# The front of a hybrid conv/DeltaNet layer: adaLN vectors in three column parts, the first scale summed by TensorE, the rows of x scaled ahead, four strips opened on the first part

## The chip, the cores and the metric

One core of one Trainium2 chip runs one program. The engines are TensorE (PE, with its weight loads PEld), VectorE (DVE), ScalarE (ACT), GpSimd (POOL) and SyncE (SP), which issues most transfers. The metric is the device time of one execution in microseconds. All inputs and the output are float32 in HBM.

## The reference

The layer takes x (2048 rows of 1024) and a vector c. Six vectors of 1024 come from `silu(c) @ w_ada + b_ada`; the first two of them, with a gain, shift and scale the normalized rows of x ahead of the large product with `w_in`:

```python
c_act = jax.nn.silu(c)
mod = c_act @ w_ada[layer] + b_ada[layer]
shift_m, scale_m, gate_m, shift_f, scale_f, gate_f = jnp.split(mod, N_MOD, axis=-1)
h = adaln(x, g_norm_mix[layer], shift_m, scale_m)     # rms_norm(x, gain) * (1 + scale) + shift
p = h @ w_in[layer]
gate_b, gate_c, h_conv, q, k, v, z, a, bt = jnp.split(p, split_at, axis=-1)
...
ya = gate_b * causal_depthwise_conv(gate_c * h_conv, conv_w_mix[layer])     # then a group norm
qkv = jax.nn.silu(causal_depthwise_conv(jnp.concatenate([q, k, v], axis=-1), conv_w_qkv[layer]))
...
o = chunked_gated_delta_rule(q, k, v, g_dec, beta)    # g_dec and beta from a and bt, per row and head
y = jnp.concatenate([ya, yb], axis=-1) @ w_out[layer]  # yb: o, normalized, times silu(z)
x = x + gate_m[:, None, :] * y
h = adaln(x, g_norm_ffn[layer], shift_f, scale_f)
x = x + gate_f[:, None, :] * ((jax.nn.silu(gt) * up) @ w_down[layer])
return adaln(x, g_norm_final, shift_o, scale_o)
```

## The kernel before

The sequence is cut into four blocks of 512 rows. In each block the mixing stage computes, for every strip of 128 columns of `w_in`, a product over eight k rows of 128 (`proj`, line 321 through `dmm`): the transposed, normalized h is held as two float32r tiles, `hTh` and `hTl` (a rounded part and the rest), the weight strip as `whi` and `wlo` (`split_w`, lines 388 and 390), and each k takes three matmuls of 128x512, so a strip takes 24. I call these the dense matmuls. The strips come in the order k, q, v, z (four heads each), then twelve for the convolution branch, then the product with `w_out`. Behind the mixing stage stand the feed-forward products.

Beside the dense matmuls run side chains, written as generators and resumed from `tick`: `head_chain` (the decay values `g` from a small product with the columns `wab`, then per head a masked k k^T), `q_chain`, `v_chain`, `diagonal_chain`, a triangular solve on VectorE that goes through DRAM twice, `level_chain`, `chunk_chain` (the recurrence over four chunks of a block) and `out_chain`, whose results (`ybs`) the third of the four steps of the product with `w_out` waits for.

A planner, `Clock`, sets the order. It keeps an estimated time for every instruction as it is recorded (`note`), decides from it when a side chain is resumed, and from the point at which `pinned` is set, each engine's instructions are put in order of these estimated times (`pin`). For a transfer it reckons 1.2 us, then bytes over a rate, then 0.8 us; the rate is line 140's. Before `pinned` is set the program's order counts, as the tile framework schedules it. `pinned` is set in block 0 when the q strips begin.

Banks of PSUM come from two pools of four, `dense_ps` (`pd`) and `misc_ps` (`pm`). The dense strips use the first; side chains, transposes and small sums use the second.

The front is everything ahead of block 0's loop. `Gm` (1 + scale, times gain) and `Sm` (shift) are needed as columns of 128 values, one per k. `part_norm` (line 726) does this in two column parts, k 0 to 4 and k 5 to 7. For each part `part_mod` (line 705) loads eight row pieces of `w_ada` (128 x 640, then 128 x 384), and VectorE multiplies each by one value of `cs` = silu(c) per partition and adds it to `acc` (lines 711, 713); `col_sums` (line 465) sums over partitions with a TensorE product with ones (line 468, two passes a call). This is done first for scale, then for shift. Every second piece also takes one step of `load_norm_steps` (line 530): load 128 rows of x, sum their squares (line 521), two small POOL steps (lines 515, 516) and scale them (line 537). Then `transpose_k` (line 544) turns x for one k through TensorE, and `scale_split` (lines 548 to 550) applies `Gm` and `Sm` and splits the result into `hTh` and `hTl`.

After the first part the small product with `wab` (`proj_ab`, lines 751 and 752) runs over k 0 to 4, and strips 0 and 1 of head group k do so too (`part_proj`, line 743); strips 2 and 3 follow behind the second part's preparation. `pre` holds the opened strips; block 0's loop finishes them over k 5 to 7. The first four `wlo` are made by VectorE once and by POOL three times (`lo_engines`).

Of the kernel before, what the change touches and what calls it, by code (L numbers as in the profile page):

```python
# [53 lines left out]
class Clock:  # L54
# [74 lines left out]
    def note(self, i):  # L129
# [9 lines left out]
        if op == "DMACopy":  # L139
            cost = min(a.free_size() * a.partition_size() for a in outs + ins) * 4 / 240e3  # L140
            begin = self.fit([eng], start, 0.45) - 0.45
# [68 lines left out]
def layer_kernel(ctx, tc, x, c, w_ada, b_ada, w_ada_final, b_ada_final, g_norm_mix, g_norm_ffn, g_norm_final,  # L210
# [19 lines left out]
    def dense_ps():  # L230
        return pd.tile([P, 512], F32, name="pd")
# [233 lines left out]
    def col_sums(acc, n):  # L465
        ps = dense_ps()
        for j in range(n):
            mm(ps[:, j * 16:(j + 1) * 16], acc[:, j * P:(j + 1) * P], ones[:, :16], start=True, stop=True)
        return ps[:, :n * 16].rearrange("p (j n) -> p j n", n=16)[:, :, 0]
# [71 lines left out]
    def transpose_k(tiles, k):  # L541
        ps = misc_ps()
        for i in range(CH):
            nc.tensor.transpose(ps[:, i * P:(i + 1) * P], tiles[i][:, k * P:(k + 1) * P], ident)
        return ps
# [126 lines left out]
    with ExitStack() as actx:  # L672
# [27 lines left out]

        xt0, pre = [], []
        xsteps = load_norm_steps([x[i * P:(i + 1) * P, :] for i in range(CH)], ap_, "kq", xt0)

        def part_mod(c0, js, slots):
            n = len(js) * P
            acc = ap_.tile([P, D], F32, name="zs" if c0 else "gate_m")[:, :n]
            for k in range(KD):
                raw = next(slots)[:, :n]
                nc.sync.dma_start(raw, w_ada[k * P:(k + 1) * P, c0 + js[0] * P:c0 + js[0] * P + n])
                if k == 0:  # L710
                    nc.vector.tensor_scalar_mul(acc, raw, cs[:, 0:1])
                else:
                    nc.vector.scalar_tensor_tensor(acc, raw, cs[:, k:k + 1], acc, op0=ALU.mult, op1=ALU.add)
                if k % 2:
                    next(xsteps, None)
            return acc

        def part_slots(names):
            while True:
                for n in names:  # L720
                    if n == "wraw":
                        yield wr.tile([P, D], F32, name=n)
                    elif n == "ym":
                        yield ap_.tile([P, BLK], F32, name=n, bufs=8)
                    else:
                        yield ap_.tile([P, D], F32, name=n)

        def part_norm(js, names):
            g, sh = Gm[:, js[0]:js[-1] + 1], Sm[:, js[0]:js[-1] + 1]
            b_g, gain, b_s = (col[n][:, js[0]:js[-1] + 1] for n in ("b_cm", "g_mix", "b_sm"))  # L730
            slots = part_slots(names)
            nc.scalar.copy(g, col_sums(part_mod(D, js, slots), len(js)))
            nc.gpsimd.tensor_add(g, g, b_g)
            nc.gpsimd.tensor_scalar_add(g, g, 1.0)
            nc.gpsimd.tensor_mul(g, g, gain)
            acc = part_mod(0, js, slots)
            if not pre:
                fill(4)
            early = [transpose_k(xt0, k) for k in js[:3]]
            nc.vector.tensor_add(sh, col_sums(acc, len(js)), b_s)  # L740
            for i, k in enumerate(js):
                scale_split(early[i] if i < len(early) else transpose_k(xt0, k), k, Gm, Sm, *hT)

        def part_proj(h):
            pre.append((ready.popleft(), dense_ps()))
            clock.kept.add(pre[-1][1].name)
            proj(pre[h][1], pre[h][0], *hT, ks=range(5))

# [4 lines left out]

        lo_engines.extend([nc.vector] + [nc.gpsimd] * 3)
        big = ["kd", "vt", "yah", "yal"]
        part_norm(range(5), ["wraw"] * 4 + big)

# [4 lines left out]
        nc.gpsimd.tensor_sub(wabs[:, :, 8:16], wab, wabs[:, :, 0:8].bitcast(F32))  # L762

        ps_ab = misc_ps()
        clock.kept.add(ps_ab.name)
        proj_ab(ps_ab, range(5))
        for h in range(2):
            part_proj(h)
        part_norm(range(5, KD), ["ym"] * 8 + big)
        for h in range(2, NH):  # L770
            part_proj(h)
        nc.sync.dma_start(ck[:, P:], cst[:, P:])
# [19 lines left out]
        for b in range(NB):  # L792
# [382 lines left out]
            if b:  # L1175
                ps_ab = misc_ps()
            proj_ab(ps_ab, range(0 if b else 5, KD))
            clock.kept.discard(ps_ab.name)
# [3 lines left out]
            for key, c0, dstT in (("k", 2048, kT), ("q", 1536, qT), ("v", 2560, None)):  # L1182
                clock.pinned = clock.pinned or key == "q"
                for h in range(NH):
                    m = (c0 - 1536) // P + h
                    if pre:
                        w, ps = pre.pop(0)
                        proj(ps, w, hh, hl, range(5, KD))
                        clock.kept.discard(ps.name)
                        fill(h + 1)  # L1190
                    else:
                        w, ps = next_w(), dense_ps()
                        proj(ps, w, hh, hl)
# [637 lines left out]
```

## Time and profile before

| | |
|---|---|
| three timed runs | 2441.77, 2443.42, 2444.44 us (median 2443.42) |
| profiled execution | 2441.17 us, of which the span from the first to the last instruction is 2439.4 |
| mean granted TensorE clock | 0.985 |
| moved | 336.98 MB, mean 138 GB/s |

A row of the page's first part is an engine's busy time, its share of the span and its instructions. In a table by stage a row gives the stretch, its length, busy time and instructions of each engine named, the granted clock, the share of the DMA engines and GB/s. In the timeline a row is the start, the time it took, engine, line, operation, output and inputs with their shapes, the count of merged instructions, and in brackets the idle time before it and what ended it. A wait is given as who waited for whom, the total, the number of times and the longest. Matmul times overlap, so the pace of a stream is read from start to start.

### The profile page before, as it was taken

Reading aid. Unit: us, or ns where it says so; the run is one execution under the profiler, and the core shown is the slowest. Engines: PE = TensorE matmul, PEld = TensorE weight load, DVE = VectorE, ACT = ScalarE, POOL = GpSimd, SP = SyncE. Lnnn points to the kernel's source line nnn. Section 1 sums busy time; section 2 is a strip of 40 time slices with the busy share of each in tenths; the row PEclk is TensorE's granted clock in tenths of the full one; section 3 lists DMA queues with packets and bytes.
Section 4 is the critical chain, followed back from the end, with each engine's and each line's share of the span. In section 5 each row is a group of like instructions: output and inputs, shape, how many; then the busy total and the mean of one; then the engine's idle time right before and its main releaser. Section 6 shows DMA issues by size and latency. Waiting matters only on the chain. (4 is left out here: it accounts for less than half of the span.)

```text
span 2439.4 us, 30808 instructions
## 1 busy us (share of the span) xinstructions
PE 2344.2 (96%) x11243; PEld 1935.6 (79%) x11243; DVE 1769.4 (73%) x2577; ACT 1044.8 (43%) x1841; POOL 592.6 (24%) x655
## 2 busy tenths in 40 slices
PE   5899899999999999988999999999999999999997
PEld 4688788887888788876878888878888877888786
DVE  5788669886887687777565565876656558878887
ACT  4543554344644474346543333533333323323345
POOL 2340344033602261221000000000000035434448
PEclk9899999999999999998999999999999999999999
DMA  7443355625562346136673243753333364333433
GB/s 249 112 117 87 95 173 158 183 95 151 152 160 87 113 121 161 51 123 196 193 226 117 87 120 99 246 168 106 108 92 116 100 240 156 117 115 126 134 132 144
DMA packets 397535, 336.98 MB, mean 138 GB/s; under 512 B 39476, under 2 KB 338749, under 8 KB 397383
## 3 DMA queue, kind: packets, MB, share of 16 engines
q1 hardware_dynamic: 397126, 334.91, 45.1%
q8 instruction: 88, 1.44, 0.2%
q14 instruction: 65, 0.52, 0.1%
q10 hardware_dynamic: 256, 0.10, 0.0%
HBM read 261.55 MB, written 73.41 MB: 137 GB/s over the span
## 5 line engine op out<-in xcount | busy, mean ns | idle before, releaser
L388 ACT CAST whi<-wraw 128x1024 fp32r<-128x1024 f32 x278 | 291.5, 1049 | 379.9 <-PE pd L321 180.7
L390 DVE TENSOR_TENSOR wlo<-wraw,whi 128x1024 fp32r<-128x1024 f32 x275 | 339.6, 1236 | 109.3 <-ACT whi L388 101.7
L321 PE MATMUL pd<-hTh,whi 128*128 128x512 f32 x896 | 365.2, 408 | 3.5 <-ACT hTh L549 2.6
L321 PE MATMUL pd<-hTl,whi 128*128 128x512 f32 x896 | 351.6, 392 | 2.7 <-DVE hTl L550 2.7
L321 PE MATMUL pd<-hTh,wlo 128*128 128x512 f32 x896 | 351.7, 392 | 0.0
L321 PEld LDWEIGHTS pd<-hTh,whi 128*128 128x128 f32 x896 | 169.7, 190 | 36.4 <-ACT hTh L549 2.7
L321 PEld LDWEIGHTS pd<-hTh,wlo 128*128 128x128 f32 x896 | 169.2, 189 | 36.5
L321 PEld LDWEIGHTS pd<-hTl,whi 128*128 128x128 f32 x896 | 170.0, 190 | 34.2 <-DVE hTl L550 3.1
L1505 POOL TENSOR_TENSOR wraw<-wraw 128x1024 f32<-128x1024 f32 x2 | 4.9, 2468 | 780.3 <-DMA wraw<-in_w_down_dram 780.3
L1459 DVE TENSOR_TENSOR sg<-sg,pd 128x512 f32<-128x512 f32 x44 | 30.2, 687 | 171.4 <-PE pd L321 165.0
L1699 DVE TENSOR_TENSOR acc<-acc,pd 128x512 f32<-128x512 f32 x192 | 127.5, 679 | 30.8 <-PE pd L321 30.8
L1582 ACT CAST xh<-ra 128x640 fp32r<-128x640 f32 (+1 forms) x88 | 62.5, 719 | 185.7 <-PE pm L321 142.8
L1160 DVE SCALAR_TENSOR_TENSOR cv<-pd,pcb,cv 128x511 f32<-128x511 f32 (+2 forms) x176 | 131.5, 747 | 4.9
L1591 POOL TENSOR_TENSOR xl<-ra,xh 128x640 fp32r<-128x640 f32 (+1 forms) x40 | 66.1, 1654 | 160.8 <-ACT xh L1582 160.8
L1699 DVE TENSOR_TENSOR acc<-acc,pm 128x512 f32<-128x512 f32 x120 | 81.6, 681 | 18.4 <-PE pm L321 17.8
L1299 POOL TENSOR_TENSOR cv<-cv,cb 128x512 f32<-128x512 f32 x32 | 52.2, 1644 | 164.7 <-DVE cv L1298 140.3
L321 PE MATMUL pd<-whi,ym 128*128 128x512 f32 x256 | 87.9, 404 | 1.5 <-ACT ym L1149 1.5
L1628 POOL TENSOR_TENSOR wraw<-wraw 128x512 f32<-128x512 f32 x40 | 69.6, 1761 | 43.3 <-DMA wraw<-in_w_down_dram 32.6
L321 PE MATMUL pd<-S2h,whi 128*128 128x512 f32 x176 | 69.5, 395 | 3.1 <-ACT whi L388 3.1
L321 PE MATMUL pd<-S3h,t3h 128*128 128x512 f32 x176 | 69.0, 392 | 2.9 <-ACT sg L1445 2.9
L321 PE MATMUL pd<-S2h,wlo 128*128 128x512 f32 x176 | 69.6, 396 | 2.2 <-DVE wlo L390 2.2
L321 PE MATMUL pd<-A22h,whi 128*128 128x512 f32 x176 | 69.6, 395 | 2.3 <-DVE sg L1459 2.2
(457 smaller groups left out, 6228.0 us busy)
## 6 DMA issues: line engine op xcount, KB each, us to landing
wraw<-in_w_in_dram SPq DMA_DIRECT2D x112, 512.0 KB, 4.0
wraw<-in_w_gate_up_dram SPq DMA_DIRECT2D x88, 512.0 KB, 3.7
ra<-act SPq DMA_DIRECT2D x80, 448.0 KB, 3.8
act<-S SPq DMA_DIRECT2D x80, 256.0 KB, 2.2
act<-act SPq DMA_DIRECT2D x68, 256.0 KB, 2.2
wraw<-in_w_ada_dram SPq DMA_DIRECT2D x32, 512.0 KB, 3.7
wraw<-in_w_out_dram SPq DMA_DIRECT2D x32, 512.0 KB, 3.8
wraw<-in_w_down_dram SPq DMA_DIRECT2D x22, 512.0 KB, 3.8
```

What stands on the lines that cost most here:

```text
L321: mm(*args, **kw)
L388: nc.scalar.copy(hi, raw)
L390: (lo_engines.popleft() if lo_engines else nc.vector).tensor_sub(lo, raw, hi.bitcast(F32))
L1160: nc.vector.scalar_tensor_tensor(cv[:, n - t:], u[:, :BLK - n + t], taps[t], cv[:, n - t:], op0=ALU.mult, op1=ALU.add)
L1299: nc.gpsimd.tensor_add(yo, yo, xr)
L1459: nc.vector.tensor_add(s5[i], s5[i], a[i])
L1505: nc.gpsimd.tensor_mul(r, r, first_w["gate"])
L1582: nc.scalar.copy(hi, raw[:, c0:c1, :])
L1591: eng.tensor_sub(lo, raw, hi.bitcast(F32))
L1628: nc.gpsimd.tensor_mul(r[:, hs], r[:, hs], gate_f[:, hs])
L1699: nc.vector.tensor_add(accs[s, u][:, ns], accs[s, u][:, ns], ps)
```

## The change

The front is written anew. There are three column parts: k 0 to 2, 3 to 5, 6 and 7. In the first part the scale is not summed by VectorE: for each piece of `w_ada` TensorE multiplies three 128x128 blocks with one column of `cs` and adds up over the eight pieces in PSUM. The other sums are made as before. `Gm` is finished by two VectorE operations instead of a copy on ScalarE and three steps on POOL. The rows of x are loaded ahead of and behind the first eight pieces, and their squares are summed and scaled in one go (`x_norm`). All transposes of a part stand ahead of its `Sm`. The four strips of head group k are all opened on the first part and continued on the second, and `proj_ab` runs over k 0 to 5 behind the second part. All four first `wlo` are VectorE's. `col_sums` takes its bank from `misc_ps`. The planner's rate for transfers goes from 240 to 380, `pinned` is set at the k strips instead of the q strips, and block 0's first q strip takes a bank of `misc_ps`.

```diff
-            cost = min(a.free_size() * a.partition_size() for a in outs + ins) * 4 / 240e3
+            cost = min(a.free_size() * a.partition_size() for a in outs + ins) * 4 / 380e3
...
     def col_sums(acc, n):
-        ps = dense_ps()
+        ps = misc_ps()
...
+        PARTS = range(3), range(3, 6), range(6, KD)
+        pre = []
+        pairs = [ap_.tile([P, 2, D], F32, name="kq", bufs=2) for _ in range(2)]
+        xt0 = [pairs[i // 2][:, i % 2, :] for i in range(CH)]
+
+        def x_load(i):
+            nc.sync.dma_start(xt0[i], x[i * P:(i + 1) * P, :])
+
+        def x_norm():
+            ss = []
+            for i in range(CH + 1):
+                if i < CH:
+                    ss.append(sum_squares(xt0[i]))
+                if i:
+                    nc.scalar.activation(xt0[i - 1], xt0[i - 1], AF.Identity, scale=ss[i - 1])
+
+        def part_slots():
+            while True:
+                for _ in range(8):
+                    yield ap_.tile([P, BLK], F32, name="ym", bufs=8)
+                for n in ("kd", "vt", "yah", "yal"):
+                    t = ap_.tile([P, 4, BLK], F32, name=n)
+                    for i in range(4):
+                        yield t[:, i]
+
+        def part_raw(c0, js):
+            for k in range(KD):
+                raw = next(slots)[:, :len(js) * P]
+                nc.sync.dma_start(raw, w_ada[k * P:(k + 1) * P, c0 + js[0] * P:c0 + (js[-1] + 1) * P])
+                yield k, raw
+
+        def part_sums(c0, js):
+            n = len(js)
+            if c0 and js[0] == 0:
+                ps = misc_ps()
+                for k, raw in part_raw(c0, js):
+                    for j in range(n):
+                        mm(ps[:, j:j + 1], raw[:, j * P:(j + 1) * P], cs[:, k:k + 1], start=k + j == 0,
+                           stop=k == KD - 1, skip_group_check=True)
+                return ps[:, :n]
+            acc = ap_.tile([P, D], F32, name="zs" if c0 else "gate_m")[:, :n * P]
+            for k, raw in part_raw(c0, js):
                 if k == 0:
                     nc.vector.tensor_scalar_mul(acc, raw, cs[:, 0:1])
                 else:
                     nc.vector.scalar_tensor_tensor(acc, raw, cs[:, k:k + 1], acc, op0=ALU.mult, op1=ALU.add)
+            return col_sums(acc, n)
+
+        def part_norm(js):
             g, sh = Gm[:, js[0]:js[-1] + 1], Sm[:, js[0]:js[-1] + 1]
             b_g, gain, b_s = (col[n][:, js[0]:js[-1] + 1] for n in ("b_cm", "g_mix", "b_sm"))
-            nc.scalar.copy(g, col_sums(part_mod(D, js, slots), len(js)))
-            nc.gpsimd.tensor_add(g, g, b_g)
-            nc.gpsimd.tensor_scalar_add(g, g, 1.0)
-            nc.gpsimd.tensor_mul(g, g, gain)
-            acc = part_mod(0, js, slots)
+            if js[0] == 0:
+                x_load(0)
+                x_load(1)
+            nc.vector.tensor_add(g, part_sums(D, js), b_g)
+            nc.vector.scalar_tensor_tensor(g, g, 1.0, gain, op0=ALU.add, op1=ALU.mult)
+            if js[0] == 0:
+                x_load(2)
+                x_load(3)
+                x_norm()
+            sums = part_sums(0, js)
             if not pre:
-                fill(4)
-            early = [transpose_k(xt0, k) for k in js[:3]]
-            nc.vector.tensor_add(sh, col_sums(acc, len(js)), b_s)
-            for i, k in enumerate(js):
-                scale_split(early[i] if i < len(early) else transpose_k(xt0, k), k, Gm, Sm, *hT)
+                fill(NH)
+            early = [transpose_k(xt0, k) for k in js]
+            nc.vector.tensor_add(sh, sums, b_s)
+            for ps, k in zip(early, js):
+                scale_split(ps, k, Gm, Sm, *hT)
...
-        lo_engines.extend([nc.vector] + [nc.gpsimd] * 3)
-        big = ["kd", "vt", "yah", "yal"]
-        part_norm(range(5), ["wraw"] * 4 + big)
+        slots = part_slots()
+        lo_engines.extend([nc.vector] * 4)
+        part_norm(PARTS[0])
+        for h in range(NH):
+            part_start()
+            proj(pre[h][1], pre[h][0], *hT, ks=PARTS[0])
+        part_norm(PARTS[1])
...
+        for h in range(NH):
+            proj(pre[h][1], pre[h][0], *hT, ks=PARTS[1])
         ps_ab = misc_ps()
         clock.kept.add(ps_ab.name)
-        proj_ab(ps_ab, range(5))
-        for h in range(2):
-            part_proj(h)
-        part_norm(range(5, KD), ["ym"] * 8 + big)
-        for h in range(2, NH):
-            part_proj(h)
+        proj_ab(ps_ab, range(6))
+        part_norm(PARTS[2])
...
-            proj_ab(ps_ab, range(0 if b else 5, KD))
+            proj_ab(ps_ab, range(0 if b else 6, KD))
...
-                clock.pinned = clock.pinned or key == "q"
+                clock.pinned = clock.pinned or key == "k"
...
-                        proj(ps, w, hh, hl, range(5, KD))
+                        proj(ps, w, hh, hl, PARTS[2])
...
-                        w, ps = next_w(), dense_ps()
+                        w, ps = next_w(), misc_ps() if b == 0 and key == "q" and h < 1 else dense_ps()
```

The change moves instructions at three places that matter below. In these rows a name like `L544` is the line, then come operation, output and inputs, shape of the output and count.

TensorE at the opening, before (`kq` holds the rows of x, `zs` and `gate_m` the sums for scale and shift, `pd` and `pm` are PSUM banks):

```order
L362 MATMUL pm<-ck,ht 128x64
L544 MATMUL pm<-ck,kq 128x128 x12
L468 MATMUL pd<-ones_r,zs 128x16 x5
L544 MATMUL pm<-ck,kq 128x128 x4
L468 MATMUL pd<-ones_r,gate_m 128x16 x5
L321 MATMUL pd<-hTh,whi 128x512 x2
```

and with the change, the same stretch (line 738 is the product in `part_sums`, `ym` a piece of `w_ada`):

```order
L362 MATMUL pm<-ck,ht 128x64
L738 MATMUL pm<-cs,ym 128x1 x24
L468 MATMUL pm<-ones_r,gate_m 128x16 x3
L544 MATMUL pm<-ck,kq 128x128 x12
L321 MATMUL pd<-hTh,whi 128x512 x2
```

The transposes have moved behind the column sums of shift, and the 24 narrow products stand in place of the scale's column sums.

VectorE at the decay chain of block 0, before (`cv` is a strip's convolution, `sp_*` and `g` the decay values, `wlo` a weight strip's lower part):

```order
L845 COPY cv<-pm 16x512
L454 SCALAR_TENSOR_TENSOR wraw<-wraw,cs 128x1024
L885 RECIPROCAL beta<-beta 128x16
L1158 TENSOR_SCALAR cv<-pd,pcb 128x512
L866 TENSOR_SCALAR sp_s<-sp_e 128x16
L390 TENSOR_TENSOR wlo<-wraw,whi 128x1024
L867 RECIPROCAL sp_s<-sp_s 128x16
L1160 SCALAR_TENSOR_TENSOR cv<-pd,pcb,cv 128x511
L868 TENSOR_TENSOR sp_s<-sp_s,sp_e 128x16
L390 TENSOR_TENSOR wlo<-wraw,whi 128x1024
L870 TENSOR_TENSOR sp_z<-sp_s 128x16
```

and with the change (25 more lines stand ahead of the loop, so line 866 is 891 now):

```order
L870 COPY cv<-pm 16x512
L1183 TENSOR_SCALAR cv<-pd,pcb 128x512
L1185 SCALAR_TENSOR_TENSOR cv<-pd,pcb,cv 128x511
L891 TENSOR_SCALAR sp_s<-sp_e 128x16
L892 RECIPROCAL sp_s<-sp_s 128x16
L893 TENSOR_TENSOR sp_s<-sp_s,sp_e 128x16
L895 TENSOR_TENSOR sp_z<-sp_s 128x16
L897 TENSOR_SCALAR sp_p<-sp_z 128x16
L899 SCALAR_TENSOR_TENSOR sp_p<-sp_p,sp_z 128x16 x7
L900 SCALAR_TENSOR_TENSOR sp_p<-sp_p,sp_s 128x16
```

The small operations stand together; the convolutions and the `wlo` that were between them come behind.

TensorE at the end of block 0, before (`ch` is a chunk's intermediate, `ym` an output of `out_chain`; the last row is the transpose in the last chunk's `out_chain`, line 1143):

```order
L1116 MATMUL pm<-ch,kd 128x128 x4
L1118 MATMUL pm<-ch,E 128x128 x4
L321 MATMUL pd<-whi,ym 128x512
L321 MATMUL pd<-wlo,ym 128x512
L321 MATMUL pd<-whi,ym 128x512 x2
L321 MATMUL pd<-wlo,ym 128x512
L321 MATMUL pd<-whi,ym 128x512 x2
L321 MATMUL pd<-wlo,ym 128x512
L321 MATMUL pd<-whi,ym 128x512
L1143 MATMUL pm<-ck,ch 128x128 x4
```

and with the change (that transpose is line 1168 now):

```order
L1168 MATMUL pm<-ck,ch 128x128 x4
L321 MATMUL pd<-whi,ym 128x512
L321 MATMUL pd<-wlo,ym 128x512
L321 MATMUL pd<-whi,ym 128x512
L1141 MATMUL pm<-ch,kd 128x128 x4
L1143 MATMUL pm<-ch,E 128x128 x4
L321 MATMUL pd<-whi,ym 128x512
L321 MATMUL pd<-wlo,ym 128x512
L321 MATMUL pd<-whi,ym 128x512
L1168 MATMUL pm<-ck,ch 128x128 x4
```

Three dense matmuls instead of nine stand between the last chunk's products and its transpose.

More of the change, by code (lines that the diff above doesn't have):

```diff
@@ L696, in layer_kernel @@
         state = ap_.tile([P, NH * P], F32, name="state")
[L701 to L706, printed above, removed]
-            for k in range(KD):
-                raw = next(slots)[:, :n]
-                nc.sync.dma_start(raw, w_ada[k * P:(k + 1) * P, c0 + js[0] * P:c0 + js[0] * P + n])
+        PARTS = range(3), range(3, 6), range(6, KD)
[20 more added lines that the diff above has]
+        def part_raw(c0, js):
+            for k in range(KD):
+                raw = next(slots)[:, :len(js) * P]
[12 more added lines that the diff above has]
+            for k, raw in part_raw(c0, js):
                 if k == 0:
@@ L713, in part_mod, with part_start @@
                     nc.vector.scalar_tensor_tensor(acc, raw, cs[:, k:k + 1], acc, op0=ALU.mult, op1=ALU.add)
[L714 to L728, printed above, removed]
+            return col_sums(acc, n)
+        def part_norm(js):
             g, sh = Gm[:, js[0]:js[-1] + 1], Sm[:, js[0]:js[-1] + 1]
             b_g, gain, b_s = (col[n][:, js[0]:js[-1] + 1] for n in ("b_cm", "g_mix", "b_sm"))
-            slots = part_slots(names)
-            nc.scalar.copy(g, col_sums(part_mod(D, js, slots), len(js)))
-            nc.gpsimd.tensor_add(g, g, b_g)
-            nc.gpsimd.tensor_scalar_add(g, g, 1.0)
-            nc.gpsimd.tensor_mul(g, g, gain)
-            acc = part_mod(0, js, slots)
-            if not pre:
-                fill(4)
-            early = [transpose_k(xt0, k) for k in js[:3]]
-            nc.vector.tensor_add(sh, col_sums(acc, len(js)), b_s)
-            for i, k in enumerate(js):
-                scale_split(early[i] if i < len(early) else transpose_k(xt0, k), k, Gm, Sm, *hT)
-        def part_proj(h):
+            if js[0] == 0:
[8 more added lines that the diff above has]
+            sums = part_sums(0, js)
+            if not pre:
+                fill(NH)
[3 more added lines that the diff above has]
+                scale_split(ps, k, Gm, Sm, *hT)
+        def part_start():
             pre.append((ready.popleft(), dense_ps()))
             clock.kept.add(pre[-1][1].name)
-            proj(pre[h][1], pre[h][0], *hT, ks=range(5))
         def proj_ab(ps, ks):
```

## The prediction

> **What bounds the kernel now.** I read the page's busy shares first, then a table by stage of the first 102 us, then TensorE's waits there, then the timeline.
>
> ```profile
> PE 2344.2 (96%) x11243; PEld 1935.6 (79%) x11243; DVE 1769.4 (73%) x2577; ACT 1044.8 (43%) x1841; POOL 592.6 (24%) x655
> ```
> ```profile
> 0.00:32.00 32.00, 8.95 (x39) 1.00 0.97 338
> ...
> 70.30:85.00 14.70, 6.94 (x18) 0.54 0.54 150
> 85.00:101.95 16.95, 16.95 (x75) 1.00 0.11 31
> ```
> ```profile
> PE pm L544 <- ACT kq L537: 13.1, 4, 5.1
> PE pm L889 <- DVE g L878: 6.5, 1, 6.5
> ```
>
> TensorE is busy 96% of the span, so time is won only where it stands idle or slow. The stage table (columns: length, TensorE busy, granted clock, DMA share, GB/s) shows two such places: up to 32 us, where it has almost no work, and 70.3 to 85, busy 6.94 of 14.70 us at clock 0.54. The second has a cause of its own: the decay chain (`head_chain`) needs `g` from VectorE, and TensorE waits 6.5 us for it. The change touches both. I follow the kernel to one mark, the first transpose of a k strip in `head_chain` (101.95), which stands behind 177 dense matmuls, and compare the work left.
>
> ```profile
> 7.59 0.34 PE L362 MATMUL pm<-ck,ht 64*128 64x64 f32 x1 [2.29 <-DMA ht<-in_g_norm_ffn_dram]
> ...
> 18.89 2.26 PEld L468 LDWEIGHTS pd<-ones_r,zs 128*128 128x128 f32 x10
> ...
> 30.41 1.03 ACT L388 CAST whi<-wraw 128x1024 fp32r<-128x1024 f32 x1
> ...
> 31.35 0.59 ACT L549 CAST hTh<-pm 128x512 fp32r<-128x512 f32 x1
> ...
> 31.82 0.76 ACT L548 ACTIVATE pm<-pm,Sm,Gm 128x512 f32<-128x512 f32 x1
> 31.97 0.69 DVE L550 TENSOR_TENSOR hTl<-pm,hTh 128x512 fp32r<-128x512 f32 x1 [1.10 <-ACT hTh L549]
> ...
> 31.99 1.22 PE L321 MATMUL pd<-hTh,whi 128*128 128x512 f32 x2 [2.56 <-ACT hTh L549]
> 32.50 1.05 ACT L388 CAST whi<-wraw 128x1024 fp32r<-128x1024 f32 x1
> ...
> 43.17 0.42 DVE L711 TENSOR_SCALAR gate_m<-kd,cs 128x384 f32<-128x384 f32 x1
> 43.50 0.61 DVE L713 SCALAR_TENSOR_TENSOR zs<-ym,cs,zs 128x384 f32<-128x384 f32 x1
> 44.03 0.61 DVE L713 SCALAR_TENSOR_TENSOR gate_m<-vt,cs,gate_m 128x384 f32<-128x384 f32 x1
> ```
> ```profile
> 48.58 0.73 PE L468 MATMUL pd<-ones_r,zs 128*128 128x16 f32 x6
> ...
> 81.33 0.63 PE L321 MATMUL pd<-hTl,whi 128*128 128x512 f32 x1
> 81.76 0.63 PE L321 MATMUL pd<-hTh,wlo 128*128 128x512 f32 x1
> ...
> 99.45 0.39 PE L321 MATMUL pd<-hTh,whi 128*128 128x512 f32 x1
> 99.68 0.39 PE L321 MATMUL pd<-hTl,whi 128*128 128x512 f32 x1
> ...
> 101.95 0.60 PE L829 MATMUL pm<-ck,kq 128*128 128x128 f32 x4
> ```
>
> From these rows come start-to-start prices. A dense matmul: 0.43 us slow (81.33 to 81.76), 0.23 fast. A short pass with a 128x128 weight load: 2.26/10, some 0.22 slow, 0.73/6 = 0.12 fast; a call of L468 is two passes. VectorE on a 128x384 piece: 0.33 for the first, 0.53 for the others. ScalarE: cast of a strip 0.94, split cast 0.47, scale 0.68.
>
> **The change, part by part.**
>
> *First scale.* Its eight DVE steps become 24 TensorE calls with one column: 48 passes. One column is not in the trace; bounds are half of a slow pass (fast, 0.11) and a slow one, and I take slow, 0.213, since TensorE is otherwise idle there. They stand behind L362, which ends at 7.9, so 7.9 + 48 x 0.213 = 18.1. Before, its column sums ended at 18.89 + 2.26 = 21.2, and a copy and three POOL steps followed. Now two small VectorE operations make `Gm` by 18.6.
>
> *First shift.* VectorE can start at 18.6; 0.33 + 7 x 0.53 = 4.0 gives 22.7. Its data stand behind x (2.1 MB) and the scale's pieces (1.57 MB), 5.2 MB with its own:
>
> ```profile
> 2.00:10.00 8.00, 0.58 (x2) 0.36 (x2) 3.21 (x4) 2.93 (x6) 0.68 (x1) 1.00 0.96 343
> 10.00:22.00 12.00, 5.29 (x22) 4.39 (x22) 8.21 (x10) 6.24 (x9) 2.55 (x7) 1.00 1.04 404
> ```
>
> At 343 GB/s to 10 us and 404 after (last column), they land at about 16.3, so transfers are hidden; at 300 GB/s for the narrower rows they would land at 19.5, still ahead of the last step. Then six passes (24.1) and twelve transposes on TensorE, the first four ending near 25.0; ScalarE's norms of x are over by 19 and no longer on the path. Scale 0.68, a strip's cast 0.94 that ScalarE's order puts between, split 0.59: **first dense matmul at 27.5, before 31.99**.
>
> *First part on four strips.* ScalarE gives a row k every 0.68 + 0.94 + 0.47 = 2.1 us, so the last `hTh` of three is there at 31.6, `hTl` at 32.6. All four `wlo` are VectorE's now instead of one; they fall into its waits. 36 dense matmuls, slow till about 32.5, end near 38.
>
> *Second part.* VectorE begins its sums only behind that last `hTl`, at 32.6: 16 pieces of 384, four of 256 from the third part that its order mixes in, 2 x 4.0 + 1.3 = 9.4 with the ends, so 42.0. TensorE has nothing dense from 38 to there. Column sums, `Sm`: 42.9. Then 12 transposes, 12 calls of `proj_ab`, 36 dense: 1.4 + 48 x 0.227 = 12.3; I add 1.7, one slow stretch of 3.4 us, because TensorE has stood nearly idle for 3 us. The second part ends at 56.8.
>
> *Third part.* Eight passes 0.9, `Sm` and `Gm` 0.5, scale and split 1.3, the last row's split, `hTl` and calls 1.9: nothing covers this on TensorE but two calls (before, 30 dense matmuls of strips 2 and 3 did). `proj_ab` ends at 61.4, before at 59.6 (next fence: VectorE's copy at 59.65 waits for it). So the earlier start is spent again by here; but at this point 22 dense matmuls of the k strips are left, before 36.
>
> *The decay chain.*
>
> ```profile
> 59.65 0.68 DVE L845 COPY cv<-pm 16x512 f32<-16x512 f32 x1 [2.33 <-PE pm L752]
> ...
> 63.55 0.17 DVE L866 TENSOR_SCALAR sp_s<-sp_e 128x16 f32<-128x16 f32 x1 [0.15 <-ACT sp_e L862]
> ...
> 76.53 0.16 DVE L878 TENSOR_TENSOR g<-sp_p,nexpa 128x16 f32<-128x16 f32 x1
> ```
> ```profile
> 329.75 0.11 DVE L866 TENSOR_SCALAR sp_s<-sp_e 128x16 f32<-128x16 f32 x1
> ...
> 332.77 0.18 DVE L878 TENSOR_TENSOR g<-sp_p,nexpa 128x16 f32<-128x16 f32 x1
> ```
>
> ```profile
> 116.61 1.28 DVE L454 SCALAR_TENSOR_TENSOR wraw<-wraw,cs 128x1024 f32<-128x1024 f32 x1
> ...
> 132.26 0.75 DVE L1158 TENSOR_SCALAR cv<-pd,pcb 128x512 f32<-128x512 f32 x1
> ...
> 136.49 0.69 DVE L918 TENSOR_TENSOR kd<-pm,eg 128x512 f32<-128x512 f32 x1
> ```
>
> The chain's small operations alternate with convolutions here (first fence): 13.0 us from 63.55 to 76.53. The change pins the order one strip group earlier, and VectorE now has them in one piece, as in block 1 (second fence), where this takes 3.0. So `g` is there 6.5 us behind `proj_ab`; but TensorE's order has the fifth strip's `wlo` ahead of the chain's matmuls, and VectorE makes it behind the chain: 8.4. TensorE waits 2 us for that. Before, `g` was there 76.7 - 59.6 = 17.1 behind. From there to the mark remain 78 dense, eight decay matmuls and six small ones, 86 x 0.227 + 0.5 = 20.0; before 25.2, because of the slow clock. VectorE needs 4.2 us for a strip's convolution and `wlo` (132.26 to 136.49) and at most 1.2 for a gate step, TensorE 24 x 0.227 = 5.4, and the first q strip takes a bank of the other pool, so the late convolutions hold up nothing. Mark: 61.4 + 8.4 + 20.0 = 89.8; with 0.7 for the chance of a slow stretch, 90.5, **11.5 earlier**.
>
> *The planner's transfer price* (240 to 380) reorders blocks 0 to 2; block 3's TensorE order around its chains is as before. I price blocks 1 and 2 at nothing, between -3 and +5: by the waits over the whole span TensorE's frequent wait there, for `kT`, was 0.6 us at most.
>
> ```profile
> PE pm L829 <- ACT kq L1198: 2.0, 4, 0.6
> ```
>
> Block 0's end I price:
>
>
> ```profile
> 264.30 3.35 DVE L1232 RECIPROCAL cv<-cv 128x512 f32<-128x512 f32 x1
> ```
> ```profile
> 275.82 2.17 ACT L537 ACTIVATE kq<-kq,ss 128x1024 f32<-128x1024 f32 x2
> ```
> ```profile
> 279.31 1.11 PE L1143 MATMUL pm<-ck,ch 128*128 128x128 f32 x4 [5.72 <-POOL ch L1138]
> ```
>
> The last chunk's output ends on a chain of VectorE, ScalarE and POOL that TensorE awaits. Now the reciprocal comes ahead of that chunk's first step (some 1.3 us shown to TensorE), three norm steps of x precede its squares instead of following (near 1), and 3 instead of 9 dense matmuls cover it (1.4): 3 us, bounds 0 and 6. Sum: -11.5 + 3.0 = **-8.5**.
>
> **The clock.**
>
> ```profile
> 40.00:44.00 4.00, 2.94 (x7) 1.55 (x8) 4.00 (x8) 0.00 (x0) 0.00 (x0) 0.59 0.71 222
> 44.00:48.00 4.00, 4.00 (x18) 2.64 (x17) 3.86 (x8) 0.00 (x0) 0.00 (x0) 0.98 0.53 122
> ```
>
> TensorE came out of a wait here (busy 2.94 of the first 4 us, so at work from about 41.1), and its granted clock was 0.59 in the first stretch and 0.98 in the second: some 3.3 us of work to the full clock. The short passes at 18.9 to 21.2 us were slow, but ran for 2.3 us only. The Trainium skill, "TensorE: Matmul & The Clock Gate", Part 1, says that the clock is halved by default, that about 3.4 us of sustained matmul activity release it, and that an idle window of that length halves it again. The rows agree with that for dense matmuls; whether passes that load 128x128 weights for one column count as such activity, no row shows. If they do, the first scale ends as the first rival has it, if not, as in the sum.
>
> **The rivals.**
> - *The short passes speed up.* Slow for 3.3 us (15 passes), then fast: 7.9 + 3.3 + 33 x 0.12 = 15.2, and all behind comes 2.9 earlier, since the pieces of the shift are there by 16.3: 2432.0. For it: TensorE has work without a break there. Against it: a single column. Chance 0.2.
> - *VectorE bounds block 0* (slower). It is busy 75.06 of the 92.90 us from 59.6 to the solve's first transfer at 152.5 (row below). With the 17.84 us of idle time that it had, starting 1.8 later, the chain is 1.8 later; TensorE then gives its lead back at the block's end and waits 3 longer: +4.8, 2448.2. It decides if VectorE idles over 16 us there; I count 3. Chance 0.09.
> - *The lead is lost in part*, at block ends or to waits of a too hopeful transfer price: -4 to +3, near 2443. Chance 0.16.
> - *Block 0's end gains instead*, with its 5.7 us wait gone: -16, near 2427. Chance 0.1.
>
> ```profile
> 59.60:152.50 92.90, 83.98 (x396) 68.31 (x395) 75.06 (x127) 48.23 (x109) 37.85 (x45) 0.93 0.41 112
> ```
>
> **How the numbers follow.** The profiled execution took 2441.17 us (span 2439.4), 2.25 under the median 2443.42. 2441.17 - 8.5 = 2432.7; on the median 2434.9, so **2434.9**, chance 0.45. With the first rival and my own bounds the range is 2426 to 2443. A measurement here tells 0.2% (4.9 us) from no change: faster 0.75, same 0.16, slower 0.09.
>
> **What would show it.** Right: first dense matmul near 27.5, a TensorE gap near 39 to 42 and a short one near 58, `g` some 6.5 us behind `proj_ab`, the mark near 90, a wait of 7 to 9 us at the end of block 0. Wrong: short passes over 0.25 us, `Sm` of the second part behind 45, clock 0.5 for long between 42 and 60, or new waits over 2 us in blocks 1 and 2.

## The result, and the profile after

The change made the kernel slower: 2451.63 us median of five runs (2450.39 to 2453.77) against 2441.77 (2440.18 to 2444.44), ratio 1.0041, 95% interval 1.0028 to 1.0055. The forecast was 2434.9, range 2426 to 2443.

The first row of the page, after:

```profile
PE 2358.5 (96%) x11285; PEld 1947.5 (79%) x11285; DVE 1778.5 (73%) x2595; ACT 1046.8 (43%) x1841; POOL 578.0 (24%) x646
```

TensorE is busy 14.3 us longer with 42 more instructions. The share doesn't tell where time was won or lost, so I number the dense matmuls (0 to 9023) by their start and take, for each number, the start after minus the start before, in one profiled execution of each kernel. Negative is ahead. A block has 864 of them: 28 strips of 24, then 192 of the product with `w_out`. Side work changes places between them, so this is read at four places: at 168 (seven strips of block 0 done, four k and three q), 740 (in block 0's product with `w_out`), 2340 (in block 2's last strips) and at the last. At the very ends of blocks 0 and 2 (864 and 2592) it reads -0.6 and +11.7, as at 740 and 2340.

```text
                       at 168   168->740   740->2340   2340->last   at last
after minus before      -7.3      +6.6       +12.5        +0.2       +12.1
```

So the front won 7.3 us, block 0's end gave 6.6 back, and blocks 1 and 2 lost 12.5. In all the kernel is 12.1 us later in the profiled pair (9.9 in the medians), where 8.5 earlier was forecast. The error of 20.6 us is 12.5 from blocks 1 and 2, forecast at nothing, 4.2 from the front and 3.6 from block 0's end, but for 0.3.

The front, TensorE's timeline after (start, time taken, operation, in brackets the wait before it):

```profile
7.76 10.40 PE L738 MATMUL pm<-cs,ym 128*128 128x1 f32 x48 [0.25 <-ACT cs L375]
23.60 1.46 PE L468 MATMUL pm<-ones_r,gate_m 128*128 128x16 f32 x6 [5.43 <-DVE gate_m L746]
28.28 1.22 PE L321 MATMUL pd<-hTh,whi 128*128 128x512 f32 x2 [0.58 <-ACT hTh L549]
...
43.39 0.81 PE L468 MATMUL pm<-ones_r,gate_m 128*128 128x16 f32 x6 [2.67 <-DVE gate_m L746]
...
57.75 0.39 PE L776 MATMUL pm<-hTl,wabs 128*16 128x512 f32 x1
...
61.45 0.61 PE L775 MATMUL pm<-hTh,wabs 128*16 128x512 f32 x1 [1.53 <-ACT hTh L549]
```
```profile
73.01 0.50 PE L321 MATMUL pm<-hTh,wlo 128*128 128x512 f32 x1 [2.44 <-DVE wlo L390]
```

VectorE's, and the stage table at the third part and behind the decay chain (length, then busy time of PE, PEld, DVE, ACT, POOL, granted clock, DMA share, GB/s):

```profile
64.23 0.68 DVE L870 COPY cv<-pm 16x512 f32<-16x512 f32 x1 [1.51 <-PE pm L776]
...
70.35 0.18 DVE L903 TENSOR_TENSOR g<-sp_p,nexpa 128x16 f32<-128x16 f32 x1
```
```profile
57.90:61.40 3.50, 2.02 (x19) 1.79 (x17) 0.39 (x3) 1.93 (x4) 0.00 (x0) 1.00 0.01 2
61.40:64.20 2.80, 2.75 (x7) 1.56 (x8) 1.29 (x2) 0.60 (x2) 0.00 (x0) 0.50 0.00 0
75.00:78.40 3.40, 3.40 (x10) 2.63 (x9) 3.40 (x4) 3.36 (x5) 1.93 (x1) 0.50 0.78 211
```

The front follows the forecast within some 1.5 us up to its third part (compared below). The end of block 0 doesn't. ScalarE's timeline, then TensorE's:

```profile
264.38 1.06 ACT L521 ACTIVATE ht<-kq 128x1024 bf16<-128x1024 f32 x1
...
265.44 1.13 ACT L537 ACTIVATE kq<-kq,ss 128x1024 f32<-128x1024 f32 x1
266.48 0.56 ACT L1174 CAST ym<-pm 128x512 fp32r<-128x512 f32 x1
```
```profile
261.77 0.60 PE L1168 MATMUL pm<-ck,ch 128*128 128x128 f32 x4
267.09 0.80 PE L321 MATMUL pd<-whi,ym 128*128 128x512 f32 x1 [4.72 <-ACT ym L1174]
...
278.00 1.11 PE L1168 MATMUL pm<-ck,ch 128*128 128x128 f32 x4 [4.72 <-POOL ch L1163]
```

The third chunk's cast of `ym` stands in ScalarE's order behind four sums of squares and a scaling of the next block's x, and TensorE waits 4.72 us for it. That wait is new; the known one for `ch` is 4.72 instead of 5.72.

In block 1 TensorE waits for the transposes of `cv` (a v strip's convolution). VectorE after, then TensorE after, then SyncE's issues after:

```profile
411.20 0.21 DVE L980 TENSOR_TENSOR lv<-yal 128x31 f32<-128x31 f32 x1 [4.01 <-DMA yal<-dm]
...
413.18 0.75 DVE L1183 TENSOR_SCALAR cv<-pd,pcb 128x512 f32<-128x512 f32 x1
```
```profile
407.28 0.66 PE L854 MATMUL pm<-ck,cv 128*128 128x128 f32 x4 [2.96 <-ACT cv L1223]
...
418.45 0.66 PE L854 MATMUL pm<-ck,cv 128*128 128x128 f32 x4 [2.79 <-ACT cv L1223]
```
```profile
398.83 0.37 SPq L966 DMA_DIRECT2D dm<-Dg  x1
...
402.31 3.47 SPq L971 DMA_DIRECT2D yal<-dm  x2
```

The same places before, VectorE and SyncE:

```profile
406.42 0.20 DVE L955 TENSOR_TENSOR lv<-yal 128x31 f32<-128x31 f32 x1
...
408.79 0.75 DVE L1158 TENSOR_SCALAR cv<-pd,pcb 128x512 f32<-128x512 f32 x1
```
```profile
395.00 0.37 SPq L941 DMA_DIRECT2D dm<-Dg  x1
...
398.37 1.22 SPq L946 DMA_DIRECT2D yal<-dm  x2
```

Before, the solve's load of `yal` was issued at 398.37 and had landed when VectorE came to it at 406.42. After, the store `dm` ahead of it came 3.8 us later and the load 3.9, while VectorE's order still put its first use at about 407: VectorE stood 4.01 us, the convolution of the next v strip began at 413.18 instead of 408.79, and TensorE waited 2.79 us for it. From 740 to 2340 TensorE's waits add up to 12.6 us after and 3.6 before, those for `cv` alone to 7.5 and 0.7; behind the wait at 418.45 it also ran 3.4 us at a granted clock of 0.50, about 1.7 us more. The load of `yal` explains that one wait; what made the others late stays open.

### The profile page after: what moved, and what is told of

Same layout as the page of the kernel before. It is cut to its first block, busy times and chain, and to the rows that moved or that the text cites. A ratio compares the mean times of both kernels' runs of the same rounds, so it can differ in the third digit from the quotient of the medians.

```text
span 2451.5 us, 30920 instructions
## 1 busy us (share of the span) xinstructions
PE 2358.5 (96%) x11285; PEld 1947.5 (79%) x11285; DVE 1778.5 (73%) x2595; ACT 1046.8 (43%) x1841; POOL 578.0 (24%) x646
## 5 line engine op out<-in xcount | busy, mean ns | idle before, releaser
L390 DVE TENSOR_TENSOR wlo<-wraw,whi 128x1024 fp32r<-128x1024 f32 x278 | 345.4, 1243 | 109.9 <-ACT whi L388 107.2
L1724 DVE TENSOR_TENSOR acc<-acc,pm 128x512 f32<-128x512 f32 x120 | 81.5, 680 | 18.1 <-PE pm L321 17.6
L321 PE MATMUL pm<-S4h,whi 128*128 128x512 f32 x176 | 68.9, 391 | 1.1 <-ACT sg L1478 1.1
```

Of the source, the lines that this page charges most:

```text
L321: mm(*args, **kw)
L390: (lo_engines.popleft() if lo_engines else nc.vector).tensor_sub(lo, raw, hi.bitcast(F32))
L1724: nc.vector.tensor_add(accs[s, u][:, ns], accs[s, u][:, ns], ps)
```

## The experiments

In each, "at 168", "740 to 2340" and so on are the columns of the table above against the kernel before. Each has its own runs of the kernel before beside it, so ratios are compared, not medians.

**The planner's rate, alone and undone.** The first run takes it back in the changed kernel, the second puts it alone into the kernel before.

```diff
 r240, the changed kernel
-            cost = min(a.free_size() * a.partition_size() for a in outs + ins) * 4 / 380e3
+            cost = min(a.free_size() * a.partition_size() for a in outs + ins) * 4 / 240e3
 old_rate380, the kernel before: the reverse
```

> The changed kernel with the planner's transfer rate back at 240. Theory P (the price): the order of blocks 1 and 2 follows from the rate alone, and the 12.5 us that the changed kernel loses between its dense matmul 740 (0.6 us ahead of the kernel before) and 2340 (11.9 behind) are the new order's; with 240 this loss is within 2 us of nothing, its waits for the conv tile cv in block 1 (2.96 and 2.79 us) and block 2 are gone, and the kernel takes some 2439 us, give or take 5 for the end of block 0, whose order changes too. Rival L (the lead): whatever starts block 0 earlier is paid back in blocks 1 and 2 because VectorE or the transfers aren't there earlier; then the loss between 740 and 2340 stays above 8 us and the kernel takes 2447 or more.

> The kernel before with nothing changed but the planner's transfer rate, 240 to 380. Theory P: the loss of some 12.5 us between dense matmul 740 and 2340 appears here too, without any change of the front, and the kernel takes some 2454 us; the waits for cv behind the solve's first transfer in block 1 appear. Rival L: without an earlier start there is nothing to give back, and the kernel takes 2440 to 2444 us.

Measured: with 240 the new kernel takes 2430.48 us, ratio 0.9953 (0.9938 to 0.9968); 380 alone makes the old kernel 2456.64, ratio 1.0058 (1.0043 to 1.0073). From 740 to 2340 they lose 1.8 and 10.0 us. By the waits from 380 to 415 us, TensorE in r240 waits at most 0.6 us for one transpose at that place in block 1 (`kq` in these rows is `kT`):

```profile
PE pm L854 <- ACT kq L1223: 0.6, 1, 0.6
PE pm L854 <- ACT cv L1223: 0.2, 1, 0.2
```

and the old kernel at 380 shows the changed kernel's pair, on VectorE and TensorE:

```profile
414.23 0.21 DVE L955 TENSOR_TENSOR lv<-yal 128x31 f32<-128x31 f32 x1 [4.02 <-DMA yal<-dm]
```
```profile
421.48 1.12 PE L829 MATMUL pm<-ck,cv 128*128 128x128 f32 x4 [3.48 <-ACT cv L1198]
```

The loss in blocks 1 and 2 belongs to the rate: it goes with it and comes with it, whatever the front. Rival L falls. The old kernel loses 10.0 and not 12.5; its order at 380 isn't quite the changed kernel's. It follows too that the rest of the change is a gain of 0.47%, more than theory P had expected, since block 0 won 4.5 us at this rate.

**The end of block 0 and the bank.**

```diff
-                        w, ps = next_w(), misc_ps() if b == 0 and key == "q" and h < 1 else dense_ps()
+                        w, ps = next_w(), dense_ps()
```

> The changed kernel with block 0's first q strip in a bank of the dense pool as before. With it the end of block 0 is ordered as in the kernel before. Theory B (the bank): the 8.2 us lost between dense matmul 690 and 740 come with this bank, which shifts the planned times so that the norm of the next x stands ahead of the third chunk's ym cast on ScalarE; without it the new wait of 4.7 us for ym is gone and the kernel takes some 2444 us. Rival: the end of block 0 is late for the same reason as the rest, the rate, or VectorE has no room there; then 2450 to 2453 us.

> The changed kernel at rate 240 with block 0's first q strip in a bank of the dense pool as before. If the bank is what it is for, the decay chain's wait grows by some 2 us and dense matmul 168 comes 2 to 4 us later, as at 380, and the end of block 0 gives that back or not: it takes 2430 to 2436 us. Rival: as at 380, where the dense bank won 3.7 us in all because the end of block 0 was ordered as in the kernel before: 2424 to 2428 us.

Measured: at 380 the kernel takes 2447.97, ratio 1.0028 (1.0017 to 1.0038) where the changed kernel has 1.0041. That is between the two expectations. The front is 3.3 us worse (at 168: -3.9 for -7.3), block 0 better by 7.2 (168 to 740: -0.6 for +6.6), and `ym` isn't late: ScalarE's cast stands ahead of the last squares again. Blocks 1 and 2 lose 14.0, at the same rate.

```profile
264.78 0.58 ACT L1174 CAST ym<-pm 128x512 fp32r<-128x512 f32 x1 [0.38 <-DVE pm L1170]
265.26 1.06 ACT L521 ACTIVATE ht<-kq 128x1024 bf16<-128x1024 f32 x1
```

At 240 the same edit is a loss: 2441.14, ratio 0.9993 (0.9982 to 1.0004) for 0.9953. The front is 2.6 us worse as expected, but from 168 to 740 it loses 3.6 where r240 wins 4.5; I had expected 2436 at most. So theory B, that the bank makes the end of block 0 late, holds only at 380. In r240, with the bank, TensorE waits 2.0 and 1.1 us at the end of block 0, both times for `ym`; the wait for `ch` (before: 5.72) is gone. Bank and rate act there through the order they give together.

**The pin.**

```diff
-                clock.pinned = clock.pinned or key == "k"
+                clock.pinned = clock.pinned or key == "q"
```

> The changed kernel with the order pinned from the q strips on, as before, and not from the k strips. My prediction's step: the pin brings the decay chain's small VectorE operations into one piece; without it convolutions stand between them again, g comes some 13 to 17 us behind the product with wab instead of 6.5, TensorE waits 4 to 8 us more there, and the kernel takes 2455 to 2460 us. Rival: the four strips opened early leave so few convolutions to mix in that g is as early as with the pin: 2450 to 2453 us.

Measured: 2457.08, ratio 1.0056 (1.0039 to 1.0072). `g` comes at 80.09 and not at 70.35, behind convolutions and `wlo` on VectorE. TensorE stands 10.57 us; its row names no releaser, but the product that reads `g` begins as soon as `g` is done:

```profile
64.30 0.67 DVE L870 COPY cv<-pm 16x512 f32<-16x512 f32 x1
...
68.50 0.66 DVE L1185 SCALAR_TENSOR_TENSOR cv<-pd,pcb,cv 128x511 f32<-128x511 f32 x1
69.15 1.22 DVE L390 TENSOR_TENSOR wlo<-wraw,whi 128x1024 fp32r<-128x1024 f32 x1
...
80.09 0.17 DVE L903 TENSOR_TENSOR g<-sp_p,nexpa 128x16 f32<-128x16 f32 x1
```
```profile
80.35 0.58 PE L914 MATMUL pm<-g,ck 128*128 128x16 f32 x2 [10.57 <-issue]
```

At 168 it is 0.6 us behind the kernel before: without the pin the whole lead of the front is gone. This step of the prediction holds, and weighs more than any other part of the front that was tested.

**Why 380 costs: kind of transfer.** Theories: the price of the large transfers, or that of the solve's small ones.

```diff
-            cost = min(a.free_size() * a.partition_size() for a in outs + ins) * 4 / 380e3
+            size = min(a.free_size() * a.partition_size() for a in outs + ins) * 4
+            cost = size / (240e3 if size > 400e3 else 380e3)
```

> The changed kernel with the rate at 240 for transfers of 512 KB (weight strips, rows of x, later pieces of w_ada) and 380 for the smaller ones (the solve's 256 KB through DRAM among them). If the large transfers carry the loss, it falls below 4 us between dense matmul 740 and 2340 and the kernel takes 2428 to 2436 us. If the solve's transfers carry it, the waits for yal and for cv behind it in block 1 stay, the loss is 8 us or more and the kernel takes 2440 or more.

> The reverse: 380 for transfers of 512 KB, 240 for the smaller ones. If the large transfers carry the loss, it is 8 us or more and the kernel takes 2440 to 2454 us. If the solve's carry it, VectorE's wait for yal in block 1 is below 1 us, the loss below 4 and the kernel takes 2428 to 2438 us, with the end of block 0 open by 5 us.

Measured: 2439.48, ratio 0.9990 (0.9980 to 0.9999), and 2428.40, ratio 0.9944 (0.9930 to 0.9959). From 740 to 2340 both lose nothing (-0.3 and -0.6). Neither kind carries the loss alone; with either at 240 it is gone. The first run's time missed its range because it gave 4.1 us back in block 0. The second gave 3.4 back there too; it is fast because it wins 9.8 us behind 2340, of which 7.1 in block 3 (see below).

**Why 380 costs: a law of the rate, or chance of the order.** Only the number in the diff changes.

> The changed kernel with the rate at 200, below the old 240. Measured against the changed kernel at 240 (2430.5 us, loss between dense matmul 740 and 2340 of +1.9 against the kernel before). Theory H (a hopeful price puts work too early, a cautious one doesn't): at 200 the loss stays within 3 us of that at 240, and the kernel takes 2427 to 2436 us. Rival C (every other rate only shuffles the order, and any order but the one at 240 costs about as much): the loss is 6 us or more and the kernel takes 2437 or more.

> The changed kernel with the rate at 300. Theory H: the loss between dense matmul 740 and 2340 lies between those at 240 (+1.9) and 380 (+12.5), some 4 to 9 us, and the kernel takes 2434 to 2445 us. Rival C: no order among the rates; the loss is as at 380 or above, 11 us or more, or below that of 240.

> The changed kernel with the rate at 235. Loss between dense matmul 740 and 2340 against the kernel before: +1.8 at 240, +9.5 at 200, +3.6 at 300, +12.5 at 380. Theory S (systematic: the loss grows with the distance of the planned from the real transfer time, so neighbours lose alike): 0 to 4 us, 2428 to 2438 in all. Theory C (chance: each rate gives another order and with it another set of waits): the neighbours of one rate scatter by as much as the far ones, 6 us or more from the value at 240.

> The changed kernel with the rate at 250. Theory S: loss 0 to 4 us between dense matmul 740 and 2340, 2428 to 2438 us in all. Theory C: 6 us or more away from the +1.8 at 240 in at least one of 235 and 250.

> The changed kernel with the rate at 360. Theory S: a loss of 10 to 13 us between dense matmul 740 and 2340, some 2449 to 2453 us in all. Theory C: a loss of 6 us or less, or of 18 or more, in at least one of 360 and 400.

> The changed kernel with the rate at 400. Theory S: a loss of 11 to 15 us between dense matmul 740 and 2340, 2450 to 2456 us in all. Theory C: a loss of 6 us or less, or of 18 or more, in at least one of 360 and 400.

```text
rate   median us   ratio (95%)               168->740  740->2340  at last
200    2454.60     1.0047 (1.0032, 1.0062)    +15.2      +9.5      +11.6
235    2427.56     0.9936 (0.9910, 0.9963)     -2.7      +3.1      -13.6
240    2430.48     0.9953 (0.9938, 0.9968)     -4.5      +1.8      -10.6
250    2444.20     1.0010 (0.9999, 1.0022)     -2.1     +11.4       +2.5
300    2443.55     1.0009 (0.9998, 1.0020)     +8.1      +3.6       -0.8
360    2448.09     1.0028 (1.0014, 1.0041)     +5.6     +14.5       +6.2
380    2451.63     1.0041 (1.0028, 1.0055)     +6.6     +12.5      +12.1
400    2440.88     1.0002 (0.9991, 1.0014)     +2.9      +4.9       -0.0
```

For blocks 1 and 2 theory C holds: 250 loses 11.4 us beside 1.8 at 240, and 400 4.9 beside 12.5 at 380. Neither distance from 240 nor direction tells the loss. It isn't scatter of the chip: four kernels at 240 with different fronts lose 1.0, 1.8, 1.0 and 1.3 us there, four at 380 lose 12.5, 10.0, 14.0 and 13.8. From matmul 800 to 2300 the traces of the four at 240 have one order of instructions on TensorE, VectorE, ScalarE and POOL, and so do three of the four at 380, the fourth being the old kernel with 10.0. One order gives one loss within 1.5 us, and a rate draws an order. The waits differ as well: in block 1 VectorE waits for `yal` in none of 250, 360 and 400, and at 250 TensorE waits for `kT` (`kq` in the row), `kd` and `cv` instead, by its waits from 340 to 720:

```profile
PE pm L854 <- ACT kq L1223: 4.3, 5, 1.2
PE pm L854 <- DVE kd L943: 2.9, 2, 1.5
PE pm L854 <- ACT cv L1223: 2.8, 2, 2.5
```

In block 0 the three rates from 235 to 250 win 2 to 5 us and the five others lose 3 to 15; whether that is a law, eight rates can't tell. My expectations on theory H at 200 and on theory S at 250 and 400 failed; H at 300 and S at 360 missed their ranges of the loss by 0.4 and 1.5 us.

The rate draws block 3's order as well, which the columns hide. From 2592 to 3456 (block 3) the rates 200, 235 and 360 and both kernels with 380 for the large transfers alone win 4.8 to 7.1 us; every other kernel lies between -1.1 and +2.3. TensorE's largest wait there is for `cv`, in the product with `w_out`. Before, then in big_at_380:

```profile
PE pd L321 <- DVE cv L1298: 10.5, 2, 8.1
```
```profile
PE pd L322 <- DVE cv L1324: 5.2, 1, 5.2
```

**The front's first scale by VectorE.**

```diff
-            if c0 and js[0] == 0:
+            if False:
```

> The changed kernel at rate 240 with the first scale summed by VectorE as the other parts are (eight operations of 128x384 and six passes, in place of 48 short TensorE passes). Theory T (the passes are the bound): the 48 passes ran from 7.8 to 18.0 us, one every 0.217, without waiting for data, so VectorE, which stood idle until 18.1, has the scale some 4 us earlier (near 14) and the shift's sums end when their last piece lands, about 21 instead of 23.4; first dense matmul 2 to 3 us earlier than 28.1, and the kernel takes 2427 to 2429 us. Rival D (the transfers are the bound): the pieces of scale or shift land no earlier than they are used now; first dense matmul at 28 or later, 2430 to 2433 us.

> Rate 380 for transfers of 512 KB and 240 for the smaller ones, with the first scale summed by VectorE. Theory T: what VectorE wins in the front comes on top of 2428.4 us: 2425 to 2427. Rival D: 2428 to 2431.

Measured: 2432.92, ratio 0.9953 (0.9937 to 0.9970), no different from r240's 0.9953; and 2423.51, ratio 0.9914 (0.9899 to 0.9928), better than 0.9944. VectorE and TensorE in the first:

```profile
7.99 3.94 DVE L746 SCALAR_TENSOR_TENSOR zs<-ym,cs,zs 128x384 f32<-128x384 f32 x6
12.51 0.62 DVE L746 SCALAR_TENSOR_TENSOR zs<-ym,cs,zs 128x384 f32<-128x384 f32 x1 [0.59 <-DMA ym<-in_w_ada_dram]
...
14.95 0.16 DVE L756 SCALAR_TENSOR_TENSOR Gm<-Gm,pca 128x3 f32<-128x3 f32 x1
16.51 0.42 DVE L744 TENSOR_SCALAR gate_m<-kd,cs 128x384 f32<-128x384 f32 x1 [1.40 <-DMA kd<-in_w_ada_dram]
```
```profile
26.35 0.73 PE L321 MATMUL pd<-hTh,whi 128*128 128x512 f32 x2 [0.58 <-ACT hTh L549]
```

`Gm` is there at 15.1 instead of 18.4 (r240), the first dense matmul at 26.4 and 25.0 instead of 28.1 and 28.2. So the 48 TensorE passes were the bound of the opening, not the transfers: theory T. Without them the transfers come next: VectorE waits 0.59 and 1.40 us for pieces. In the first run a lead of 4.0 us over r240 stands until 2340 and is lost behind it (2340 to last +5.9, r240 -1.3). Kernels with one order there differ by that much: the four at 240 have -1.3, +5.9, -3.1, +2.3. With 1.7 to 3 us at stake in the front, the total of r240_dve_scale decides nothing, though it misses T's 2427 to 2429. The second's total is on T's side but wins more than T gave it (5.8 us over big_at_380 in the traces, 3.2 of them by 168), so the rows of the opening decide. It is the fastest kernel here, 0.86% under the kernel before. Of its 20.1 us in the profiled pair 10.5 come by 168, 6.5 in block 3 and 5.3 behind it, where the four at 240 spread from -4.9 to +4.8.

**The first wlo.**

```diff
-        lo_engines.extend([nc.vector] * 4)
+        lo_engines.extend([nc.vector] + [nc.gpsimd] * 3)
```

> The changed kernel at rate 240 with the first four wlo made by VectorE once and by POOL three times, as before. My step: VectorE's three wlo fall into its waits, so moving them to POOL wins nothing for VectorE; POOL takes some 2.4 us for each, later than TensorE wants them: dense matmul 36 is 0 to 3 us later and the kernel takes 2430 to 2433 us. Rival: VectorE's wlo delay hTl and with it the second part's sums (1.2 us each behind 28 us), so POOL frees 2 us of them: 2427 to 2429 us.

Measured: 2433.38, ratio 0.9958 (0.9942 to 0.9975), no different. Dense matmul 36 is 0.3 us earlier, not later, and 168 comes 3.1 later. That is the clock: both kernels wait 2.5 us for a `wlo` ahead of `g`'s product, but behind it the granted clock is halved here and not in r240. From 98 to 120 this kernel falls 3.2 us behind. This kernel, then r240:

```profile
75.40:82.20 6.80, 6.80 (x21) 5.54 (x20) 6.69 (x10) 3.57 (x5) 1.53 (x2) 0.50 0.54 157
```
```profile
75.40:82.20 6.80, 6.80 (x32) 5.61 (x32) 6.73 (x11) 4.24 (x7) 2.22 (x3) 1.00 0.57 159
```

## Why the prediction was wrong

*The step that failed* is the one on the planner's transfer price: "I price blocks 1 and 2 at nothing, between -3 and +5", read from the small waits of the kernel before. The new order has its own waits, and the old trace can't show them. Measured: +12.5 us, and +10.0 with the rate alone. The rival that named "a too hopeful transfer price" had the right place, with a price of +3 at most.

*Block 0's end*, +3 with bounds 0 and 6: +6.6 over the block. I priced what comes ahead of the last chunk's step. The rows of the third chunk, whose cast fell behind the next x's norm on ScalarE, I had not priced; in q_bank, where the cast isn't late, block 0 loses nothing from 168 on, so at 380 the order that comes with this bank made the loss, and no lack of room on VectorE. The wait for `ch`, forecast at 7 to 9 us, was 4.72.

*The front*, -11.5 to the mark: at the same count of dense matmuls -7.3. The first dense matmul came at 28.28 (forecast 27.5), VectorE's sums of the second part began at 33.35 (32.6), the wait for `wlo` was 2.44 (2), `g` came 6.3 us behind `proj_ab` (6.5). The 48 passes ended at 18.16 (18.1). Three things were mis-sized. The column sums of the second part's shift began at 43.39 where the sum has VectorE done at 42.0, so the part's last `proj_ab` call ended at 58.1 instead of 56.8. In the third part the wait of 1.53 us for `hTh` was in the sum (nothing covers it), but behind it TensorE ran at a granted clock of 0.50 (row 61.40:64.20), for which the sum had nothing: six matmuls 0.43 us apart instead of 0.23, another 1.2 us or so. These two make most of the 2.8 us by which `proj_ab` was late (64.2 instead of 61.4). And the slow stretch 75.00:78.40 cost some 1.7 us where the sum had 0.7 for its chance. With it 3.8 of the 4.2 us are found; the rest is the longer wait for `wlo`.

*The first rival*, short passes that speed the clock up, is out: all 48 kept one pace from 7.76 to 18.16. *VectorE bounds block 0*, the rival on the slow side, had the right sign for another reason.

*The sum without the rate* came near by luck: -8.5 forecast, and r240, which has every other part, measured -10.6 in the profile and -0.47%. Its two terms missed in opposite directions: the front won 6.7 instead of 11.5, and block 0's end won 4.5 instead of losing 3.0. At 240 the rival "Block 0's end gains instead" is what happened there. The way of the front's gain held (first dense matmul, `g` in one piece, the pin); the sizes didn't.

What stays open: why 200 and 300 to 400 lose in block 0 and 235 to 250 don't, why some orders win in block 3, and which estimate of the planner is at fault in each order.

## What to carry to other kernels

A number that feeds a planner is not a small edit: it redraws the order of work all over the kernel, and its price can't be read from the waits of the old order. Forecast it with a range as wide as the orders scatter (here 0.9936 to 1.0047 of the time before, 27 us), or test it by itself first, and judge the rest of the change at the old number. A count of one engine's main instructions, compared by number between two traces, shows where time was lost long before the waits do.

## What the runs showed of the hardware

One-column TensorE products with their weights loaded anew took 0.213 us a pass from the first to the last of 48, over 10.4 us without a break. Passes of L468 start 0.21 us apart at the slow pace (row 23.60) and 0.11 at the full one (row 43.39), so these never left the slow one. In the changed kernel's trace the dense matmuls from 28.28 on began at it too, 0.43 us apart.

The moment of the full pace in the front isn't fixed. A trace's record of the clock begins with the change to the full one, and ahead of that a row reads 1.00 whatever the pace; in the changed kernel it begins at 34.06 us. So the granted clock read 1.00 all through that slow stretch, and there the pace of the matmuls has to be read, not the clock:

```profile
30.00:32.00 2.00, 2.00 (x6) 1.52 (x6) 2.00 (x3) 1.97 (x4) 0.00 (x0) 1.00 1.06 392
32.00:34.00 2.00, 2.00 (x6) 1.61 (x5) 1.96 (x4) 0.54 (x1) 0.00 (x0) 1.00 1.14 323
34.00:36.00 2.00, 2.00 (x10) 1.60 (x9) 1.93 (x5) 0.25 (x1) 0.61 (x1) 1.00 1.01 336
```

In fourteen kernels with the same TensorE work up to the first dense matmul, the record begins between 32.2 and 34.2 us in eight and between 27.3 and 28.1 in six. In these six the first dense matmuls already ran at the full pace, as in pin_at_q (the same row took 1.22 us in the changed kernel):

```profile
28.11 0.73 PE L321 MATMUL pd<-hTh,whi 128*128 128x512 f32 x2 [0.63 <-ACT hTh L549]
```

In these six, TensorE had nothing between the 48 passes and the change but six passes of column sums and twelve transposes, which began at most 4.6 us ahead of it. So such work can bring the change, and 10.4 us of one-column passes didn't in any of the fourteen. The Trainium skill, "TensorE: Matmul & The Clock Gate", Part 1, says that the release varies by 500 ns either way between runs, since the window runs freely; the spread here is 6.9 us. In every trace the changes of the clock lie whole multiples of 3.41 us apart (changed kernel: 34.06, 44.30, 47.71, 61.37, 64.78).
